# One inference step of a hybrid decoder: the input projection as seven block products

## The chip, the cores and the metric

The kernel runs on one core of one Trainium2 chip. The metric is device microseconds of one execution, from start to end on that core; lower is better. PE is TensorE, DVE is VectorE, ACT is ScalarE, POOL is GpSimd and SP is SyncE, which here only issues DMAs.

## What is computed

One layer on 2048 prompt tokens and 32 sample tokens, width 1024, all in float32. The part that the change touches is the first product, whose result `z` is cut into six column blocks of 512:

```python
h = rms_norm(x, norm_mix_g)                 # (T, 1024)
z = h @ w_in                                # w_in: (1024, 3072)
dq, dk, dv, rq_rk, rv, rg = six blocks of 512 columns of z
dq, dk = partial_rotary(dq) / 8, partial_rotary(dk)      # differential attention
rq, rk = rotate(rq), rotate(rk) / 8                      # retention, chunks of 128 tokens
ret = retention(rq, rk, rv)                 # a state is carried from chunk to chunk
r = silu(rg) * rms_norm(ret)                # per head
```

Differential attention, the output projection, a SwiGLU FFN (width 2816) and a final norm follow. The rotated keys, the values, the retention states and the outputs of the layer are returned.

## The kernel before

Every matmul in full precision is made of three in `float32r`: an operand is split into a high part (a cast on ACT) and a low part (a subtraction on DVE), and high x high, low x high and high x low are added up in PSUM. `split` does this (lines 122 to 124).

`projection` goes over four groups `g` of 512 tokens. For a group it loads x transposed (tiles `xr`, two k-tiles of 128 features each), scales it by the norm's weight into `xh` and `xl`, and adds up squares in `sq` for the norm. Then it goes over the six column blocks in the order 1, 2, 0, 3, 4, 5 (k, v, q, retention's q and k, retention's v, gate). A block's weights come from DRAM as four pieces of 512 KB (`wr`, line 175), each split into `wh` and `wl` (six buffers each). For each of the four tiles of 128 tokens, `terms` issues 8 k-tiles x 3 = 24 matmuls of 128 x 512 into a PSUM bank `z` (lines 295 to 297). ACT and DVE take `z` on: `put_qk` scales, rotates, transposes on PE and splits, and its rows go to DRAM (`q_d`, `k_d`) on POOL's DMA queue; `put_v` stores through SP; block 3 is rotated to `rot`; block 4 starts `retention` of a tile, block 5 the gate and `gated_out`. In group 0 the 32 sample tokens ride along as a fifth tile (`sample_terms`: 16 `float32r` matmuls per block). In group 1 `sample_retention` updates the sample states, with tile `sr`.

The engines run their instructions in program order, and a scheduler sets that order for the whole program while it is built. Tiles of one name take turns in `bufs` buffers; whoever writes one next waits until its last reader is done. The FFN was already computed with seven products in place of eight. After the projection come attention (L793 to L865), the output projection (L952 to L954), `ffn_in` (L1159) and `ffn_out` (L1375).

Of the kernel before, what the change touches and what calls it, by code (L numbers as in the profile page):

```python
# [11 lines left out]
F32 = mybir.dt.float32  # L12
# [9 lines left out]
P = 128  # L22
# [23 lines left out]
class Step:  # L46
# [3 lines left out]
    def run(self):  # L50
        tc = self.tc
        with (
# [10 lines left out]
            ]  # L63
            self.xs_d = dram.tile([P, KT, NS], F32, name="xs_d")
# [78 lines left out]
    def projection(self, const):  # L143
        nc, tc, a = self.nc, self.tc, self.a
        order = (1, 2, 0, 3, 4, 5)
        with (
# [17 lines left out]
            self.state = None  # L164
            for g in range(4):
                tiles = [4 * g + i for i in range(4)] + ([NQ] if g == 0 else [])
                xh, xl = [], []
                wts = {}
                rp = pa.tile([P, 4, 160], F32, tag="rope", name="rope", bufs=2)
                self.rope_t = {4 * g + i: rp[:, i] for i in range(4)}  # L170
                self.rope_t[NQ] = rope_s

                def load_w(b, kp):
                    wr = early.tile([P, 2, 512], F32, tag="wr", name="wr", bufs=2)
                    nc.sync.dma_start(wr, a["w_in"][b, :, 2 * kp : 2 * kp + 2, :])
                    wh = pw.tile([P, 2, 512], F32R, tag="wh", name="wh", bufs=6)
                    wl = pw.tile([P, 2, 512], F32R, tag="wl", name="wl", bufs=6)
                    self.split(wh, wl, wr)
                    wts[b, kp] = (wh, wl)

                sq = early.tile([P, 2, 512], F32, tag="sq", name="sq", bufs=1)
                for kp in range(KT // 2):
                    xr = early.tile([P, 2, 512], F32, tag="xr", name="xr", bufs=2)
                    nc.sync.dma_start(xr, a["xt"][:, 2 * kp : 2 * kp + 2, 512 * g : 512 * g + 512])
                    h = px.tile([P, 2, 512], F32R, tag="xh", name="xh", bufs=5)
                    l = px.tile([P, 2, 512], F32R, tag="xl", name="xl", bufs=5)
                    for j in range(2):
                        gk = gmix[:, 2 * kp + j : 2 * kp + j + 1]
                        nc.scalar.activation(h[:, j], xr[:, j], AF.Copy, scale=gk)  # L189
                        nc.vector.scalar_tensor_tensor(  # L190
                            l[:, j], xr[:, j], gk, h[:, j].bitcast(F32), ALU.mult, ALU.subtract
                        )
                    nc.scalar.activation(sq if kp == 0 else xr, xr, AF.Square)
                    if kp:
                        nc.vector.tensor_tensor(sq, sq, xr, ALU.add)
# [1401 lines left out]
```

## Time and profile before

| | |
|---|---|
| median of 3 runs | 2719.81 us (2718.56 to 2725.04) |
| profiled execution, its own time | 2720.14 us |
| its span, first to last instruction | 2718.4 us |
| mean granted TensorE clock | 0.985 |
| projection | 0 to 679 us of the span |
| groups 0, 1, 2, 3 of it | 0 to 194, to 364, to 522, to 679 us |

The bounds of the groups are read from the timeline: the sums of squares of groups 1, 2 and 3 (`ssp`, L220) stand at 205.5, 375.6 and 533.8 us, some 12 us into a group, and the first scores of attention at 678.9. A row of a group of instructions reads: line, engine, operation, tiles written and read, shape, count | busy us, mean ns of one | idle time of the engine just before them and who ended it. A matmul's duration reaches into the next one; from start to start is what it costs. Times of rows that the prediction uses are shown there.

### The profile page before, as it was taken

The page shows a single profiled execution, that of the slowest core. Times are in us where ns is not written, and L with a number is a line of the kernel's source. Part 1 is how long each engine was busy: PE and PEld are TensorE (multiplying, and loading weights), DVE is VectorE, ACT ScalarE, POOL GpSimd, SP SyncE. Part 2 cuts the span into 40 slices and gives each one's busy share as a digit, 9 for nine tenths or more (in the row PEclk, how much of TensorE's full clock was granted, in tenths as well). Part 3 has the DMA queues.
Part 4 walks back from the last instruction along what each step waited for, and adds up shares of the span by engine and source line. Part 5 has one row for each costly group of instructions (what it writes and reads, how often), then busy time and mean ns, then how long its engine had stood idle before and what let it go on. Part 6 is the DMA issues. An engine that isn't in the chain of part 4 may idle for free.

```text
span 2718.4 us, 35500 instructions
## 1 busy us (share of the span) xinstructions
PE 2624.3 (97%) x13180; PEld 2097.5 (77%) x13180; DVE 1528.1 (56%) x2296; ACT 1065.6 (39%) x2051; POOL 1010.3 (37%) x1032
## 2 busy tenths in 40 slices
PE   8999999999898999998999999999999999999998
PEld 7777788787566788886768777787777777788886
DVE  5554544543556667776365555575766765345364
ACT  4343343432555555654243333353323333333342
POOL 1000000011562233324456555558777784003111
PEclk9999999999899999999999999999999999999999
DMA  7436555364994555624442222354434436744463
GB/s 247 129 102 189 147 156 151 107 180 128 242 249 125 143 158 141 156 79 151 147 171 87 103 101 82 109 174 171 146 129 170 144 131 208 267 142 149 142 207 120
DMA packets 166347, 413.35 MB, mean 152 GB/s; under 512 B 19376, under 2 KB 54896, under 8 KB 164384
## 3 DMA queue, kind: packets, MB, share of 16 engines
q1 hardware_dynamic: 100176, 259.63, 29.5%
q0 software_dynamic: 56784, 147.27, 18.7%
q10 hardware_dynamic: 9216, 4.20, 0.6%
q8 instruction: 104, 1.70, 0.3%
q14 instruction: 67, 0.55, 0.1%
HBM read 287.95 MB, written 123.08 MB: 151 GB/s over the span
## 4 chain that ended last, share of the span: by engine, by line
PE 79%; DVE 7%; DMA 6%; issue 3%; ACT 2%; POOL 2%; ACTq 0%; SPq 0%; POOLq 0%; DVEq 0%
PE fps L1159 22%; PE ops L1375 15%; PE z L297 7%; PE z L295 7%; PE z L296 7%; PE op L851 3%; DVE wl L124 3%; PE sp L793 2%; PE sp L796 2%; PE atp L840 2%; DMA w<-w_ffn_in 2%; PE cz L953 2%; PE cz L952 2%; PE cz L954 1%; DMA w<-w_ffn_out 1%
## 5 line engine op out<-in xcount | busy, mean ns | idle before, releaser
L1159 PE MATMUL fps<-xh,wh 128*128 128x512 f32 x1232 | 484.7, 395 | 4.1 <-ACT xh L123 4.1
L1159 PE MATMUL fps<-xh,wl 128*128 128x512 f32 x1232 | 481.8, 391 | 0.0
L1159 PE MATMUL fps<-xl,wh 128*128 128x512 f32 x1232 | 480.9, 390 | 0.0
L295 PE MATMUL z<-wh,xh 128*128 128x512 f32 x768 | 303.9, 397 | 7.8 <-ACT xh L189 7.8
L297 PE MATMUL z<-wl,xh 128*128 128x512 f32 x768 | 304.1, 397 | 0.0
L296 PE MATMUL z<-wh,xl 128*128 128x512 f32 x768 | 302.6, 394 | 0.0
L1159 PEld LDWEIGHTS fps<-xh,wh 128*128 128x128 f32 x1232 | 231.8, 188 | 70.1 <-issue 14.2
L1159 PEld LDWEIGHTS fps<-xh,wl 128*128 128x128 f32 x1232 | 231.7, 188 | 58.3 <-issue 9.2
L1159 PEld LDWEIGHTS fps<-xl,wh 128*128 128x128 f32 x1232 | 231.9, 188 | 47.1
L124 DVE TENSOR_TENSOR xl<-xl,xh 128x1024 fp32r<-128x1024 f32 (+1 forms) x133 | 149.1, 1144 | 202.0 <-ACT xh L123 201.9
L1375 PE MATMUL ops<-vh,xh 128*128 128x512 f32 x616 | 240.4, 394 | 4.8 <-ACT u L1403 2.6
L1375 PE MATMUL ops<-vh,xl 128*128 128x512 f32 x616 | 239.2, 390 | 0.0
L1375 PE MATMUL ops<-vl,xh 128*128 128x512 f32 x616 | 238.0, 390 | 0.0
L124 DVE TENSOR_TENSOR wl<-w,wh 128x512 fp32r<-128x512 f32 x132 | 158.9, 1220 | 114.9 <-ACT wh L123 114.5
L797 DVE TENSOR_REDUCE mx<-sp 128x1 f32<-128x1024 f32 (+4 forms) x192 | 168.3, 908 | 86.0 <-PE sp L796 65.6
L124 DVE TENSOR_TENSOR wl<-wt,wh 128x512 fp32r<-128x512 f32 x176 | 189.7, 1079 | 30.0 <-ACT wh L123 26.3
L123 ACT CAST xh<-xl 128x1024 fp32r<-128x1024 f32 (+1 forms) x133 | 111.5, 868 | 217.5 <-DMA xl<-hop_d 187.4
L123 ACT CAST wh<-wt 128x512 fp32r<-128x512 f32 x176 | 108.9, 621 | 190.5 <-PE fps L1159 155.6
L124 DVE TENSOR_TENSOR wl<-wr,wh 128x1024 fp32r<-128x1024 f32 x96 | 117.3, 1223 | 109.0 <-ACT wh L123 97.0
L295 PEld LDWEIGHTS z<-wh,xh 128*128 128x128 f32 x768 | 145.1, 189 | 38.0 <-ACT xh L189 7.8
L123 ACT CAST wh<-w 128x512 fp32r<-128x512 f32 x132 | 81.8, 620 | 225.8 <-PE fps L1159 175.0
L297 PEld LDWEIGHTS z<-wl,xh 128*128 128x128 f32 x768 | 144.9, 189 | 31.8 <-issue 0.7
(308 smaller groups left out, 5016.6 us busy)
## 6 DMA issues: line engine op xcount, KB each, us to landing
wr<-w_in SPq DMA_DIRECT2D x96, 512.0 KB
w<-w_ffn_in SPq DMA_DIRECT2D x44, 1024.0 KB
xl<-hop_d SPq DMA_DIRECT2D x77, 512.0 KB
hop_d<-so POOLq DMA_DIRECT2D x88, 256.0 KB
kst<-k_d POOLq DMA_DIRECT2D x36, 512.0 KB
hop_d<-h POOLq DMA_DIRECT2D x66, 256.0 KB
qd<-q_d POOLq DMA_DIRECT2D x64, 256.0 KB
xop_d<-xt POOLq DMA_DIRECT2D x56, 256.0 KB
```

The costliest lines, as they stand in the source:

```text
L123: nc.scalar.copy(hi, src)
L124: nc.vector.tensor_tensor(lo, src, hi.bitcast(F32), ALU.subtract)
L295: mm(z, h[:, j, c], wh[:, j], start=k == 0, stop=False)
L296: mm(z, l[:, j, c], wh[:, j], start=False, stop=False)
L297: mm(z, h[:, j, c], wl[:, j], start=False, stop=k == KT - 1)
L793: nc.tensor.matmul(sp[:, o : o + nn], q[:, 2 * mp, sl], k, start=True, stop=False)
L796: nc.tensor.matmul(sp[:, o : o + nn], q[:, 2 * mp + 1, sl], k, start=False, stop=True)
L797: nc.vector.tensor_reduce(mx[:, c : c + 1], sp[:, :w], AX.X, ALU.max, negate=True)
L840: nc.tensor.transpose(tp[:, j, :], pt[b // 8][0][:, P * (b % 8) : P * (b % 8) + P], self.ident)
L851: self.nc.tensor.matmul(st["o"], ats[(b - lo) // 4][:, (b - lo) % 4, :], vs[b // 4][:, b % 4, :], start=b == 0, stop=b == st["i"],)
L1159: i = nc.tensor.matmul(bank, w[:, c], v, start=first and k == 0 and n == 0, stop=k == half - 1 and n == 2, skip_group_check=True,)
L1375: nc.tensor.matmul(bank, x[:, c], w, start=first and n == 0, stop=end and n == 2, skip_group_check=True)
```

## The change

The input projection is computed with one level of Strassen's scheme (seven products of half size in place of eight). A group's x (512 tokens x 1024 features) is a 2 x 2 matrix of blocks: tokens in halves of 256, features in halves of four k-tiles. The weights of two column blocks (`pairs`: 1 with 2, 0 with 3, 4 with 5) are the other 2 x 2 matrix: the same halves of features, and the two blocks. A `product` is two token tiles x 4 k-tiles x 3 = 24 matmuls of 128 x 512.

- x: `xr` now holds k-tile k and k + 4. DVE scales it in place; `a` (the two blocks a11 and a12, for products 0 and 1) and `b` (a22, product 3) are split off; POOL forms four sums in place; `c` (products 5 and 2) and `d` (products 6 and 4) are split from them. Each of the eight operand tiles has one buffer.
- Weights: products 0, 1 and 2 read `w_in` as before. Products 4, 3, 6 and 5 read four sums of weight blocks from a new DRAM tensor `tin_d`, straight into the buffer of `wl`, where ACT and DVE split them.
- `prepare` makes these sums, in group 0 only: for each pair, k-tile k and half of the columns it loads four blocks of 128 x 256 into `wq` (two buffers), uses them at once for the sample tokens (fp32 matmuls with 32 rows, the four blocks on four strips of the bank `zsp`), then POOL subtracts four times in place and stores the four results to `tin_d`. That is 24 such chunks of 512 KB. `prepare` for the first pair stands ahead of the products, for the next pairs behind product 1 of the pair before.
- Results: products 0, 5 and 4 are kept (`u`, `v`), and DVE adds them to the other products out of PSUM (`f`), POOL makes one more sum per pair of tiles. `put` takes on what the loop's branches did before. A pair's products run in the order 0, 1, 5, 4, 2, 6, 3.
- To make room in SBUF: `wh`, `wl` five buffers for six, `qkh`, `qkl` 256 tokens for 512, `vrow`, `rt`, `sm`, `rope` and `sr` one buffer for two, `ro` three for four.

```diff
+            self.tin_d = [dram.tile([P, 4, KT // 2, 512], F32, name=f"tin_d{p}") for p in range(3)]
...
-        order = (1, 2, 0, 3, 4, 5)
+        pairs = ((1, 2), (0, 3), (4, 5))
+        half = KT // 2
...
+            where = {0: ("a", 0), 1: ("a", 1), 3: ("b", 0), 5: ("c", 0), 2: ("c", 1), 6: ("d", 0), 4: ("d", 1)}
+            def weights(bp, o, wts):
+                b, c = pairs[bp]
+                for k in (0, 2):
+                    h = pw.tile([P, 2, 512], F32R, tag="wh", name="wh", bufs=5)
+                    l = pw.tile([P, 2, 512], F32R, tag="wl", name="wl", bufs=5)
+                    if o < 3:
+                        i = k + (half if o else 0)
+                        src = a["w_in"][c if o == 2 else b, :, i : i + 2, :]
+                    else:
+                        src = self.tin_d[bp][:, {4: 0, 3: 1, 6: 2, 5: 3}[o], k : k + 2, :]
+                    r = early.tile([P, 2, 512], F32, tag="wr", name="wr", bufs=2) if o < 3 else l.bitcast(F32)
+                    nc.sync.dma_start(r, src)
+                    self.split(h, l, r)
+                    wts[o, k // 2] = (h, l)
...
+            def prepare(sap, xs, bp):
+                b, c = pairs[bp]
+                z = ps.tile([P, 512], F32, tag="r", name="zsp", bufs=2)
+                for k in range(half):
+                    for n in range(2):
+                        cols = slice(256 * n, 256 * n + 256)
+                        w = sap.tile([P, 2, 2, 256], F32, tag="wq", name="wq", bufs=2)
+                        for e in range(2):
+                            nc.sync.dma_start(w[:, e], a["w_in"][pairs[bp][e], :, k : k + half + 1 : half, cols])
+                        for e in range(2):
+                            for i in range(2):
+                                q = 2 * e + i
+                                nc.tensor.matmul(
+                                    z[32 * q : 32 * q + 32, cols],
+                                    xs[:, k + half * i, :],
+                                    w[:, e, i, :],
...
+                        w11, w21, w12, w22 = w[:, 0, 0], w[:, 0, 1], w[:, 1, 0], w[:, 1, 1]
+                        padd(w11, w12, w11, ALU.subtract)
+                        padd(w12, w22, w12, ALU.subtract)
+                        padd(w22, w22, w11, ALU.subtract)
+                        padd(w21, w21, w22, ALU.subtract)
+                        nc.gpsimd.dma_start(
+                            self.tin_d[bp][:, :, k, cols], w.rearrange("p e i c -> p (e i) c")
+                        )
...
+                for n, m in (("a", 2), ("b", 1), ("c", 2), ("d", 2)):
+                    x[n] = [px.tile([P, m, half, 256], F32R, tag=f"x{i}{n}", name=f"x{i}{n}") for i in "hl"]
+                for k in range(half):
+                    xr = load_x(g, k)
...
+                    xh, xl = x["a"]
+                    self.split(xh[:, :, k], xl[:, :, k], xr[:, :, :256])
+                    a11, a21, a12, a22 = xr[:, 0, :256], xr[:, 0, 256:], xr[:, 1, :256], xr[:, 1, 256:]
+                    xh, xl = x["b"]
+                    self.split(xh[:, 0, k], xl[:, 0, k], a22)
+                    padd(a22, a21, a22, ALU.add)
+                    padd(a21, a11, a21, ALU.subtract)
+                    padd(a11, a22, a11, ALU.subtract)
+                    padd(a12, a12, a11, ALU.subtract)
+                    for n, cols in (("c", slice(0, 256)), ("d", slice(256, 512))):
+                        xh, xl = x[n]
+                        self.split(xh[:, :, k], xl[:, :, k], xr[:, :, cols])
...
+                    for p in range(2):
+                        product(0, p, z[p], x, wts, True, False)
+                        u.append(line("u", 2))
+                        nc.scalar.copy(u[p], z[p])
...
+                        product(1, p, z[p], x, wts, False, True)
+                        out(b, p, z[p])
+                    if g == 0 and bp < 2:
+                        zsn = prepare(sap, xs, bp + 1)
+                    weights(bp, 5, wts)
...
+                        product(3, p, z[p], x, wts, False, True)
+                        f = line("f", 2)
+                        add(f, z[p], u[p], ALU.add)
+                        out(b, 2 + p, f)
...
-        vr = self.early.tile([P, 512], F32, tag="vrow", name="vrow", bufs=2)
+        vr = self.early.tile([P, 512], F32, tag="vrow", name="vrow", bufs=1)
...
-            sr = pool.tile([P, NH, P], F32, tag="sr", name="sr", bufs=2)
+            sr = pool.tile([P, NH, P], F32, tag="sr", name="sr", bufs=1)
```

How it moves the instructions, at three places. A row of the order has line, operation, tiles written and read, shape, and what it waits for (DMAHW: a DMA that SP issued, DMASW: one that POOL issued, else an engine).

PE, group 0, where the first column block's tiles end (before): the sample tile (`xs`) follows on weights that are in SBUF already, and the next block's first tile after it.

```order
L307 MATMUL z_514<-wh_307,xs_318 64x512
L308 MATMUL z_514<-wl_308,xs_318 64x512
L307 MATMUL z_514<-wh_307,xs_318 64x512
L308 MATMUL z_514<-wl_308,xs_318 64x512
L295 MATMUL z_572<-wh_550,xh_249 128x512 [waits Activation_49]
L296 MATMUL z_572<-wh_550,xl_250 128x512
L297 MATMUL z_572<-wl_551,xh_249 128x512
L295 MATMUL z_572<-wh_550,xh_249 128x512
```

PE, group 0, first pair (after), ahead of the second half of product 5 (`wh_688`): `wq_587` and `wq_599` are the first two chunks of the second pair.

```order
L218 MATMUL zsp_586<-wq_587,xsr_372 32x256
L218 MATMUL zsp_586<-wq_599,xsr_372 32x256 [waits DMAHW2_49]
L218 MATMUL zsp_586<-wq_599,xsr_372 32x256
L218 MATMUL zsp_586<-wq_599,xsr_372 32x256 [waits DMAHW3_49]
L218 MATMUL zsp_586<-wq_599,xsr_372 32x256
L197 MATMUL z_693<-wh_688,xhc_253 128x512 [waits Activation_49]
L197 MATMUL z_693<-wh_688,xlc_254 128x512
L197 MATMUL z_707<-wh_688,xhc_253 128x512
L197 MATMUL z_707<-wh_688,xlc_254 128x512
L197 MATMUL z_693<-wl_689,xhc_253 128x512 [waits DVE_49]
```

Where weights in SBUF were all that PE took, it now stands behind a strip matmul for each load of a chunk.

SP, first DMAs of group 0 (before): x and weights, each behind a buffer that ACT and DVE have read.

```order
L175 DMA wr_289<-w_in 128x1024 [waits DMAHW1_49,DVE_49]
L184 DMA xr_279<-xt 128x2x512 [waits DMAHW0_49,DVE_49]
L175 DMA wr_305<-w_in 128x1024 [waits DMAHW3_49,DVE_49]
L184 DMA xr_295<-xt 128x2x512 [waits DVE_49]
L175 DMA wr_548<-w_in 128x1024 [waits DMAHW5_49,DVE_49]
L175 DMA wr_554<-w_in 128x1024 [waits DMAHW7_49,DMAHW2_49,DVE_49]
```

SP, group 0 (after): `wl_684` and `wl_689` are the two halves of product 5's weights, `wq_*` chunks of `prepare`.

```order
L214 DMA wq_438<-w_in 128x2x256 [waits DMAHW2_49,DMAHW1_49,DMASW5_49]
L214 DMA wq_438<-w_in 128x2x256
L186 DMA wl_684<-tin_d0_89 128x1024 [waits DMAHW3_49]
L214 DMA wq_450<-w_in 128x2x256 [waits DMAHW5_49,DMAHW4_49,DMAHW6_49,DMASW2_49,Pool_49]
L214 DMA wq_450<-w_in 128x2x256
L214 DMA wq_462<-w_in 128x2x256 [waits DMAHW1_49,DMAHW2_49,DMASW3_49,Pool_49]
L214 DMA wq_462<-w_in 128x2x256 [waits DMAHW7_49]
L214 DMA wq_587<-w_in 128x2x256 [waits DMAHW4_49,DMAHW0_49,DMAHW5_49,DMASW4_49,Pool_49]
L214 DMA wq_587<-w_in 128x2x256
L214 DMA wq_599<-w_in 128x2x256 [waits DMAHW6_49,DMAHW7_49,DMASW5_49,Pool_49]
L214 DMA wq_599<-w_in 128x2x256 [waits DMAHW3_49]
L186 DMA wl_689<-tin_d0_89 128x1024 [waits PE_49]
```

Loads of chunks now wait for POOL and for earlier stores from its queue (DMASW), and the reads of `tin_d` are queued behind them.

DVE, end of a group and begin of the next (before, groups 0 to 1): x of the next group is split beside the last rows of the sample tile.

```order
L190 SCALAR_TENSOR_TENSOR xl_1685<-xr_1682,gmix_179,xh_1684 128x512 [waits DMAHW5_49,Activation_49]
L373 SCALAR_TENSOR_TENSOR ro_1402<-ro_1402,rss_1597,gate_1595 128x128 [waits Pool_49]
L373 SCALAR_TENSOR_TENSOR ro_1402<-ro_1402,rss_1597,gate_1595 128x128 [waits DVE_49]
L373 SCALAR_TENSOR_TENSOR ro_1402<-ro_1402,rss_1597,gate_1595 128x128 x2
L190 SCALAR_TENSOR_TENSOR xl_1685<-xr_1682,gmix_179,xh_1684 128x512 [waits Activation_49]
L190 SCALAR_TENSOR_TENSOR xl_3005<-xr_3002,gmix_179,xh_3004 128x512 [waits DMAHW6_49,Activation_49]
L312 TENSOR_TENSOR zs_1627<-z_1610,zs_1627 32x512 [waits DVE_49]
L190 SCALAR_TENSOR_TENSOR xl_3005<-xr_3002,gmix_179,xh_3004 128x512 [waits Activation_49]
L462 TENSOR_TENSOR skd_1920<-rot_s_216,sdec_1889 32x4x64 [waits DMAHW3_49]
L462 TENSOR_TENSOR skd_1920<-rot_s_216,sdec_1889 32x4x64
L124 TENSOR_TENSOR wl_2041<-wr_2038,wh_2040 128x1024 [waits DMAHW7_49,Activation_49]
```

DVE, the same place (after, groups 2 to 3): `f_4772` is the last eviction of product 3, `xlb_4832` the first write to the `b` operand of the next group.

```order
L394 TENSOR_TENSOR f_4772<-z_4637,u_4368 128x512 [waits PE_49,Pool_49]
L125 TENSOR_TENSOR xlb_4832<-xr_4838,xhb_4831 128x256 [waits Activation_49]
L125 TENSOR_TENSOR xlb_4832<-xr_4871,xhb_4831 128x256 [waits Activation_49]
L119 TENSOR_SCALAR rss_4623<-rss_4623 128x4 [waits Activation_49]
L492 TENSOR_TENSOR sm_4715<-sp_4716,rmask_244 128x2x128 [waits DVE_49,PE_49]
L492 TENSOR_TENSOR sm_4715<-sp_4717,rmask_244 128x2x128 [waits PE_49]
L522 TENSOR_TENSOR ro_4744<-op_4724,rdec_246 128x2x128 [waits PE_49]
L125 TENSOR_TENSOR wl_5052<-wl_5052,wh_5051 128x1024 [waits DMAHW1_49,Activation_49]
L472 SCALAR_TENSOR_TENSOR ro_4485<-ro_4485,rss_4623,gate_4621 128x128 [waits Pool_49]
L472 SCALAR_TENSOR_TENSOR ro_4485<-ro_4485,rss_4623,gate_4621 128x128 [waits DVE_49]
```

The rest of the x operands of group 3 follows over the next 36 rows, up to the `xla` of k-tile 3, with retention of the last two tiles between them. Before, the buffers of x let its split run ahead of the last matmuls; now `b`, `c` and `d` come behind them.

More of the change, by code (lines that the diff above doesn't have):

```diff
@@ L165, in projection @@
             for g in range(4):
[L166 to L169, printed above, removed]
+                wts, x = {}, {}
+                rp = pa.tile([P, 4, 160], F32, tag="rope", name="rope", bufs=1)
                 self.rope_t = {4 * g + i: rp[:, i] for i in range(4)}
                 self.rope_t[NQ] = rope_s
[L173 to L179, printed above, removed]
```

242 lines of the change are left out of this document (136 added, 106 removed).

## The prediction

> **What bounds the kernel now.** I read the page first (engine shares), then the busy time by stage, the groups of instructions of the projection, and last the timeline at single places.
>
> ```profile
> span 2718.4 us, 35500 instructions
> PE 2624.3 (97%) x13180; PEld 2097.5 (77%) x13180; DVE 1528.1 (56%) x2296; ACT 1065.6 (39%) x2051; POOL 1010.3 (37%) x1032
> ```
>
> The same profiled execution took 2720.14 us, so 1.7 us lie outside its span; the median of the three runs is 2719.81. The sum below starts from 2720.1. The projection is all of the change. Its four token groups are four stretches of the span (columns: us, then busy us of PE, PEld, DVE, ACT, POOL, the granted clock, the DMA share, GB/s):
>
> ```profile
> 0.00:194.00 194.00, 186.23 (x893) 145.64 (x894) 99.20 (x194) 80.55 (x134) 20.59 (x33) 0.99 0.51 155
> 194.00:364.00 170.00, 169.54 (x847) 135.16 (x846) 88.81 (x191) 61.30 (x104) 13.23 (x18) 1.00 0.55 163
> 364.00:522.00 158.00, 158.00 (x769) 127.71 (x768) 74.46 (x146) 60.87 (x104) 12.58 (x17) 1.00 0.50 146
> 522.00:679.00 157.00, 157.00 (x770) 126.43 (x768) 64.14 (x134) 48.51 (x93) 21.53 (x31) 1.00 0.54 150
> ```
>
> PE is busy throughout and nothing else is near full. One idle stretch of 7.8 us stands at the start, before the first operands:
>
> ```profile
> L295 PE MATMUL z<-wh,xh 128*128 128x512 f32 x768 | 303.9, 397 | 7.8 <-ACT xh L189 7.8
> 201.39 0.39 PE L295 MATMUL z<-wh,xh 128*128 128x512 f32 x1
> 202.07 0.39 PE L295 MATMUL z<-wh,xh 128*128 128x512 f32 x1
> ```
>
> The 397 ns overlap. From 201.39 to 202.07 there are three matmuls (L295, L296, L297), so one costs 0.227 us of PE. Per group 6 blocks x 4 tiles x 8 k x 3 = 576 of them are 131 us of the 158; 27 us are transposes and retention.
>
> **What comes off PE.** Seven products of 24 matmuls replace 192 per pair: 72 fewer per group, 288 in all, 288 x 0.227 = -65.4 us (16.3 per group). The 96 sample matmuls (L307, L308) become 96 fp32 ones of 32 x 256 on strips. The same form stands in the FFN:
>
> ```profile
> L307 PE MATMUL z<-wh,xs 128*64 128x512 f32 x48 | 19.0, 396 | 0.0
> 1383.99 1.05 PE L1204 MATMUL sz<-w,xs 128*32 128x256 f32 x10
> 1384.97 0.73 PE L1159 MATMUL fps<-xh,wh 128*128 128x512 f32 x2
> ```
>
> Ten records, two to an instruction, hold PE for 0.98 us: 0.2 each, 19 us against 96 x 0.227 = 22, so -3. Half of the 32 ssp matmuls go: under -2. Gross gain 70 us, at most.
>
> **Group 0: the sums kept in DRAM.** Products 5, 4, 6 and 3 read sums that this same group must first write. `prepare` makes 24 chunks (three pairs, eight each), and a chunk's buffer goes round: two loads on SP, four strip matmuls, four dependent POOL subtractions of 256 columns, a store on POOL's queue; with two buffers the next load waits until a store has landed. The order shows the strip matmuls of the following chunks on PE ahead of product 5's second half, and SP's read of the sums behind those loads. Prices:
>
> ```profile
> 66.49 1.47 SPq L175 DMA_DIRECT2D wr<-w_in  x2
> 70.53 1.05 ACT L123 CAST wh<-wr 128x1024 fp32r<-128x1024 f32 x1 [0.87 <-DMA wr<-w_in]
> 257.66 4.17 DMA ret_sample<-sr
> 261.84 4.35 DMA sr<-state_ret
> 1300.86 0.76 POOL L1001 DMA_DIRECT2D xop_d<-xt  x1 [4.33 <-DVE xt L987]
> 1304.05 1.28 POOL L1013 TENSOR_TENSOR xt<-xt 128x512 f32<-128x512 f32 x1 [2.43 <-DMA xop_d<-xt]
> L1323 POOL TENSOR_TENSOR wt<-w 128x512 f32<-128x512 f32 x11 | 14.0, 1273 | 44.1 <-DMA w<-w_ffn_out 44.1
> L1144 POOL TENSOR_TENSOR wt<-w 128x512 f32<-128x512 f32 x44 | 69.9, 1606 | 3.9 <-DVE wl L124 3.9
> ```
>
> A 512 KB load is used 4.0 us after its issue. A 256 KB store is waited for 4.17 us (issued by SP) or 3.2 us (by POOL: 1300.86 to 1304.05); I take 3.5 for 512 KB, nearer to the POOL row, since POOL issues these. POOL's 256 columns were not run; half of 1.27 and of 1.61 bounds them by 0.64 and 0.80, I take 0.71. Both buffers go in step (POOL alternates between them), so two chunks cost 3.5 + 4.0 + 0.5 (strip matmuls) + 8 x 0.71 = 13.7 us, with bounds of 12.1 and 15.1 (POOL 0.64 and 0.80, store 3.2 and 4.17, load 4.0 and 4.35). Twelve such rounds are 164 us. The first chunk lands near 10, and some 14 us are added where POOL does the sums of x (16 x 0.71, half of it beside a landing) and stands behind the stores of q and k. The last sum is in DRAM near 188. Then 4.0 for its read, 2.3 for cast and split, and 108 matmuls (half of product 5, then 4, 2, 6, 3) of 24.5 us: group 0 ends near 219, 2 more for matmuls in the slow clock (below): 221 against 194, **+27**. By the bounds -6 to +44: 19 down and 17 up for the rounds, 14 down if all the added POOL work is hidden.
>
> The DMA queues give a second bound. Group 0 moved 194 us x 155 GB/s = 30 MB. Added are 9.4 MB of weights (42 half-megabyte loads for 24), 12.6 MB of chunk loads and 12.6 of stores: 65 MB.
>
> ```profile
> DMA packets 4337, 8.76 MB, mean 274 GB/s; under 512 B 1472, under 2 KB 1488, under 8 KB 4336
> ```
>
> That is the first 32 us, the densest stretch of the projection. 65 MB at 274 GB/s are 236 us, so a group 0 much under 200 is not to be had from this side either.
>
> After a wait PE is slow for a while:
>
> ```profile
> 1376.08 1.22 PE L1159 MATMUL fps<-xh,wh 128*128 128x512 f32 x2 [4.09 <-ACT xh L123]
> 1378.80 0.63 PE L1159 MATMUL fps<-xh,wh 128*128 128x512 f32 x1
> 1379.23 0.63 PE L1159 MATMUL fps<-xl,wh 128*128 128x512 f32 x1
> 1380.01 0.39 PE L1159 MATMUL fps<-xh,wh 128*128 128x512 f32 x1
> ```
>
> After 4.09 us idle a matmul takes 0.43 until 1379.66, then 0.23: some eight at +0.2, 1.6 us a gap. In group 0 most gaps end in another wait on the chain, which takes that up; I count one gap, 2 us. (The Trainium skill, "TensorE: Matmul & The Clock Gate", Part 1, speaks against the change here: after an idle window of about 3.4 us PE drops to half its clock and needs as much busy time to come back. The row agrees. If each of some eight gaps were paid in full, an estimate by that rule, the sum would be 12 us more than mine.)
>
> **Groups 1 to 3: the boundary.** Here the sums lie ready and PE has 141 us of work (158 - 16.3 - 0.6). DVE's rows:
>
> ```profile
> L124 DVE TENSOR_TENSOR wl<-wr,wh 128x1024 fp32r<-128x1024 f32 x96 | 117.3, 1223 | 109.0 <-ACT wh L123 97.0 <-DMA v_prompt<-vrow 11.5
> L385 DVE COPY rt<-tp 128x512 f32<-128x512 f32 x16 | 11.0, 687 | 3.6 <-PE tp L383 3.3
> L190 DVE SCALAR_TENSOR_TENSOR xl<-xr,gmix,xh 128x512 fp32r<-128x512 f32 x32 | 22.7, 745 | 2.7 <-ACT xh L189 2.7
> L195 DVE TENSOR_TENSOR sq<-sq,xr 128x1024 f32<-128x1024 f32 x12 | 14.6, 1218 | 0.2
> L601 DVE TENSOR_SCALAR dpr<-dpr,dk 128x544 f32<-128x544 f32 x2 | 1.0, 520 | 0.0
> L373 DVE SCALAR_TENSOR_TENSOR ro<-ro,rss,gate 128x128 f32<-128x128 f32 x64 | 18.2, 347 | 20.0 <-ACT gate L280 15.2 <-POOL rss L119 4.7
> L393 DVE TENSOR_TENSOR sm<-sp,rmask 128x256 f32<-128x256 f32 x32 | 13.2, 422 | 36.1 <-PE sp L391 36.1
> L415 DVE SCALAR_TENSOR_TENSOR state<-state,rdec,up 128x128 f32<-128x128 f32 x30 | 9.0, 342 | 1.1 <-PE up L409 1.1
> ```
>
> Per group 18 more splits of 1.22 (22), 24 adds out of PSUM at 0.69 (17), and for x some 19 instead of 8 x 0.745 + 3 x 1.22 = 10: +48, on about 80 (the four stretches' mean): 128 us, under PE's 141. It is not the sum that hurts but one place. The x operands have one buffer, so the next group's b operand (read by product 3, the last) is written only after the last matmul, then POOL makes c and d, then the two x buffers come free and k = 2 and 3 are loaded. The order has 50 DVE rows between the last eviction and the xla of k = 3: 3 weight splits (3.7), 12 gated rows (4.2), 8 of the sm kind (3.4), 4 states (1.4), 12 of 128x512 (8.3), 4 scalings (2.0), 3 xlb (1.3), 4 small ones (0.6): 25 us. PE has there the retention of two tiles, one of them
>
> ```profile
> 674.33 0.71 PE L391 MATMUL sp<-rt 64*128 64x128 f32 x4
> 678.89 0.38 PE L793 MATMUL sp<-kst,qd 128*128 128x256 f32 x1
> ```
>
> 4.6 us long (the next work begins at 678.89), and 18 matmuls of products 5 and 0 (4.1): 13 us. **+12** per boundary; the bounds are 0 (DVE's retention work slips behind) and +16 (its waits for ACT and DMA in between). Before, PE had 158.00 of 158 there.
>
> Small edits: five weight buffers for six, `vrow` one for two (the second v tile's eviction holds ACT until two stores have landed, some 4 us, with half a product, 2.7 us, of cover), one `rt`, one `sm`, three `ro`, two u, v and f each. The cover is the one and a half products (8 us) between a weight buffer's release and its use; a load, cast and split take 4.0 + 1.05 + 1.22. Thin: 0 to 8 us a group, taken as 3. `sr` with one buffer makes the sample states serial (4.17 + 4.35 + work, four times, some 43 us) beside a pair of 41 us of PE: 0 to 6, taken as 2. ACT gains 18 casts of 1.05 and 12 copies, some 35 us on 61: covered.
>
> Sum: +27, then 3 x (-16.9 + 12 + 3) = -6, +2: +23. 2720.1 + 23 = **2743**.
>
> **Rivals.** (1) Quick rounds: 12.1 us each (POOL 0.64, landings of 3.2 and 4.0). Group 0 ends near 202, +8; with -6 and +2, 2724: no change. For it: the POOL store row; against it: two DMA streams beside it. (The Trainium skill, "DMA: Bandwidth & Descriptors", "Anatomy of one DMA", puts a POOL-issued DMA at 2.0 us plus bytes over 436 GB/s, an estimate of 3.2 us for 512 KB: it is on this side; the 4.17 us row is above it.) (2) Faster: with quick rounds, DVE's retention rows slip behind the x operands and a boundary costs 2 and not 12. Group 0 +8, then 3 x (-16.9 + 2 + 3) = -36, and +2: 2694. It decides from boundaries under about 7 us. (3) Much slower: the DMA bound rules group 0, 236 us, +42, and the boundaries cost 16: 2720 + 42 + 6 + 2 = 2770. (4) PE is not the bound in the projection, so fewer matmuls give nothing: excluded by 158.00 of 158.
>
> **How the numbers follow.** Forecast 0.48, (1) 0.14, (2) 0.20, (3) 0.18. Within 0.3% (8 us) is what a measurement of this kernel can hardly tell from no change. Slower 0.66, same 0.14, faster 0.20. The range leaves a tenth on either side: 2692, just past (2), and 2785, past (3) by the clock's 12. Of the likeliest case alone: 2728 to 2760.
>
> **What would show it.** The ssp matmuls of group 1, at 205.5 now, come near 235; the waits name DMA wq and tin_d for PE, ACT and POOL, some 50 us of PE idle before 221. At three boundaries DVE is solid for 25 us and PE idle for 12. In between a product takes 24 x 0.227 = 5.45 us. Wrong would be: group 0 under 200, or boundaries with PE full.

## The result, and the profile after

The changed kernel took 2853.32 us in its profiled execution, 2853 to 2863 in its runs, against 2719.2 us (median) of the kernel before: a ratio of 1.0501, interval 1.0471 to 1.0531. One more run, in which the granted clock was 0.645 and not 0.947, took 3739 us and is not counted. I had predicted 2743; slower was right, by 133 us and not by 23.

The page of the changed kernel: span, busy time, and the granted clock in 40 slices of 71 us.

```profile
span 2851.5 us, 36218 instructions
PE 2637.2 (92%) x12956; PEld 2071.1 (73%) x12956; DVE 1745.0 (61%) x2543; ACT 1174.3 (41%) x2218; POOL 1229.5 (43%) x1256
PEclk7787898998979999999999999999999999999999
```

PE has 224 matmul instructions fewer and is busy 13 us *longer*. The last row tells where: in the first twelve slices, 855 us and with them the projection, the clock was down to 0.7 or 0.8 in eight, and it was at 0.9 or more in all that follow. Busy time by stage, cut at the ssp matmuls of groups 0 to 3 (their marks) and at the first attention matmul, with group 0 in three pieces, first of the changed kernel, then three of the same stretches of the kernel before (us, then busy us of PE, PEld, DVE, ACT, POOL, the granted clock, DMA share, GB/s):

```profile
0.00:42.00 42.00, 14.26 (x50) 6.22 (x50) 25.59 (x40) 16.91 (x27) 28.82 (x39) 0.80 0.69 225
42.00:125.00 83.00, 56.63 (x235) 35.80 (x236) 36.42 (x46) 22.50 (x30) 49.45 (x59) 0.69 0.68 223
125.00:246.00 121.00, 88.60 (x395) 60.24 (x394) 73.78 (x107) 39.82 (x60) 65.80 (x76) 0.81 0.74 229
246.00:318.80 72.80, 62.91 (x251) 46.45 (x250) 50.91 (x93) 33.81 (x70) 19.58 (x16) 0.76 0.46 150
318.80:491.80 173.00, 164.80 (x770) 128.21 (x768) 131.82 (x238) 87.92 (x148) 43.73 (x46) 0.94 0.63 199
491.80:657.00 165.20, 151.86 (x698) 117.96 (x698) 126.23 (x217) 87.54 (x153) 39.28 (x43) 0.94 0.63 201
657.00:815.00 158.00, 146.12 (x659) 114.36 (x658) 105.40 (x181) 72.39 (x122) 50.84 (x58) 0.92 0.75 219
```

```profile
0.00:28.50 28.50, 20.73 (x84) 17.06 (x85) 18.92 (x30) 18.78 (x24) 6.32 (x15) 1.00 0.86 283
28.50:205.50 177.00, 177.00 (x861) 138.09 (x861) 89.33 (x179) 66.88 (x115) 14.27 (x18) 0.99 0.47 140
533.80:678.90 145.10, 145.10 (x712) 116.85 (x710) 55.85 (x121) 42.53 (x78) 20.52 (x30) 1.00 0.55 151
```

Start +13.6 (42.1 for 28.5), group 0 from mark to mark +99.7 (276.7 for 177.0), groups 1 to 3 +2.9, +7.0 and +13.0: together 136 us, and nothing behind the projection. Group 0 is most of the loss; groups 1 to 3 lose where each should have gained 16.9.

What group 0 waits for (engine, waited for: us, times, longest; to 318.8 us):

```profile
ACT wh L124 <- DMA wl<-tin_d: 92.9, 22, 28.7
POOL wq L227 <- PE zsp L218: 43.7, 10, 7.2
PE zsp L218 <- DMA wq<-w_in: 41.8, 12, 9.7
SPq L214 <- DMA tin_d<-wq: 92.5, 14, 14.9
```

The longest of these, in the chain of work around it (start, us, what; rows left out are marked):

```profile
74.85 4.06 DMA wq<-w_in
...
78.95 2.77 PE zsp L218 x12
...
81.75 0.72 POOL wq L227
...
85.83 0.77 POOL wq L230
86.60 0.29 issue
86.89 3.44 DMA tin_d<-wq
...
91.62 5.83 DMA wl<-tin_d
...
97.48 1.05 ACT wh L124
...
98.58 11.17 PE z L197 x36
109.75 0.57 PE zsp L218 x8
```

That is one round of two chunks: load 4.06, strips 2.8 (at a granted clock of 0.50), POOL 5.1, store 3.44, then the next loads on SP: 15.5 us. Only then does SP issue the reads of the sums (91.62), which stood behind the chunk loads. The next strips wait behind 36 matmuls of the products (98.58 to 109.75), and POOL's subtractions with them. So it goes on to the end of group 0: the stores, SP's wait for the last of them, the reads behind it, and the last matmul of the last product.

```profile
L231 POOL DMA_DIRECT2D tin_d<-wq x24: 695/728/837, 28.8 to 242.6; - x24
SPq L186 <- DMA tin_d<-wq: 19.8, 1, 19.8
246.00 1.28 SPq L186 DMA_DIRECT2D wl<-tin_d  x3
289.49 0.39 PE L197 MATMUL z<-wl,xhb 128*128 128x512 f32 x1
```

The last of the 24 stores is issued at 242.6 and has landed at 246.0, where the forecast had 188: 19 us a round. Group 0's last product ends at 289.9.

### The profile page after: what moved, and what is told of

It reads as the page before. It is cut to its first block, busy times and chain, and to the rows that moved or that the text cites. A ratio compares the mean times of both kernels' runs of the same rounds, so it can differ in the third digit from the quotient of the medians.

```text
span 2851.5 us, 36218 instructions
## 1 busy us (share of the span) xinstructions
PE 2637.2 (92%) x12956; PEld 2071.1 (73%) x12956; DVE 1745.0 (61%) x2543; ACT 1174.3 (41%) x2218; POOL 1229.5 (43%) x1256
## 4 chain that ended last, share of the span: by engine, by line
PE 67%; DMA 12%; DVE 10%; ACT 4%; issue 4%; POOL 2%; SPq 0%; ACTq 0%; POOLq 0%; DVEq 0%
PE fps L1258 25%; PE ops L1474 14%; PE z L197 7%; DMA wl<-tin_d 4%; PE op L950 3%; DVE wl L125 3%; PE sp L892 2%; PE sp L895 2%; PE atp L939 2%; PE cz L1051 2%; PE cz L1052 2%; PE cz L1053 2%; ACT wh L124 1%; DMA w<-w_ffn_in 1%; DMA xr<-xt 1%
## 5 line engine op out<-in xcount | busy, mean ns | idle before, releaser
L125 DVE TENSOR_TENSOR wl<-wl,wh 128x1024 fp32r<-128x1024 f32 x96 | 124.1, 1295 | 129.3 <-ACT wh L124 128.1
L124 ACT CAST wh<-wl 128x1024 fp32r<-128x1024 f32 x96 | 100.6, 1048 | 188.7 <-DMA wl<-tin_d 187.6
L892 PE MATMUL sp<-kst,qd 128*128 128x512 f32 (+1 forms) x320 | 127.9, 400 | 27.0 <-ACT p L910 25.8
L950 PE MATMUL op<-vv,at 128*128 128x128 f32 x1088 | 142.4, 279 | 0.3 <-ACT at L941 0.3
L1474 PEld LDWEIGHTS ops<-vh,xh 128*128 128x128 f32 x616 | 116.1, 189 | 31.0 <-ACT u L1502 4.0
L950 PEld LDWEIGHTS op<-vv,at 128*128 128x128 f32 x1088 | 133.0, 194 | 4.7 <-issue 2.5
```

The lines of the kernel that those rows point to most:

```text
L124: nc.scalar.copy(hi, src)
L125: nc.vector.tensor_tensor(lo, src, hi.bitcast(F32), ALU.subtract)
L892: nc.tensor.matmul(sp[:, o : o + nn], q[:, 2 * mp, sl], k, start=True, stop=False)
L950: self.nc.tensor.matmul(st["o"], ats[(b - lo) // 4][:, (b - lo) % 4, :], vs[b // 4][:, b % 4, :], start=b == 0, stop=b == st["i"],)
L1474: nc.tensor.matmul(bank, x[:, c], w, start=first and n == 0, stop=end and n == 2, skip_group_check=True)
```

## Experiments

One profiled run each, beside the kernel before (2715 to 2725 us). Differences are taken from the changed kernel's 2853.3; its own runs reach from there to 2862.9, so under 10 us is not read from a total. A run's mark is the place of group 1's ssp matmuls (318.8 in the changed kernel), its periods are the times from there to the next marks and to the attention (496.3 together). Where a kernel leaves work out, its expectation says which.

**Group 0.** Reads of a tile that is always ready:

```diff
+ self.alt_d = dram.tile([P, 2, 512], F32, name="alt_d")
+ self.nc.gpsimd.dma_start(self.alt_d, self.a["w_in"][0, :, 0:2, :])
  src = self.tin_d[bp][:, {4: 0, 3: 1, 6: 2, 5: 3}[o], k : k + 2, :]
+ src = self.alt_d if g == 0 else src
```

> In group 0 the products 3 to 6 read one fixed 512 KB tile in DRAM, written once at the start, and not the sums of prepare (their values are wrong); prepare itself, its loads, strips, subtractions and stores, is as before. Theory A (the sums' way through DRAM sets the end of group 0): the reads no longer wait, group 1's ssp matmuls come 60 to 80 us earlier than the 318.8 us of the changed kernel, and the time falls to about 2785. Theory B (the strip matmuls stand in PE's order ahead of products that are ready, so PE waits for chunk loads whoever reads the sums): under 20 us earlier, 2840 to 2855. Theory C (the bytes set it): no change, 2853.

Measured 2778.8 (-75); group 1's ssp at 253.5. Theory A, and most of the loss.

```diff
- for e in range(2):
+ for e in range(2 if k == 0 else 0):
      for i in range(2):
```

> The strip matmuls run for the first two of the eight chunks of a pair only (the sample rows are wrong), everything else as in the changed kernel. Theory A: the last sum still has to come through its 24 rounds, the strips were a short link of each; 10 to 25 us less, about 2835. Theory B: PE is free of the chunk loads, the 41.8 us of waits at the strips go with the slow matmuls behind them; 45 us or more less, under 2810. Theory C: no change, 2853.

Measured 2824.1 (-29), ssp at 298.3. This lies between the two, nearer to A's 10 to 25: the strips are a link of the round, and a longer one than A had said.

Both edits at once:

> Both edits to group 0 at once: products 3 to 6 of group 0 read the fixed tile, and the strips run for two chunks of eight (sample rows and products wrong). PE is free of prepare, which goes on loading, subtracting and storing beside it. If waiting alone was the loss of group 0: group 1's ssp at 210 to 222, as without any sums (216.5). If the traffic of the loads and stores, or their place in SP's queue, costs by itself: 230 to 245.

Measured 2779.8, ssp at 234.0: in the total no better than the first edit alone, though the mark came 20 us earlier. Prepare did not get quicker; its stores were issued from the first to

```profile
L234 POOL DMA_DIRECT2D tin_d<-wq x24: 713/745/842, 33.4 to 288.5; - x24
```

that is, into group 1, which reads the sums, and there the time that group 0 had won was given back (ssp to ssp 191 us; 161 with the first edit alone). SP's queue points to why: up to 290 us it stood at weight loads whose buffer DVE (46.6 us) or PE (43.9 us) had not yet read out, and 39.3 us at stores of chunks, and the loads of chunks stood behind both.

```diff
- padd(w11, w12, w11, ALU.subtract)
...
- nc.gpsimd.dma_start(self.tin_d[bp][:, :, k, cols], ...)
- src = self.tin_d[bp][...]
+ src = self.alt_d
```

> prepare keeps its loads and its strips, but makes no sums and no stores; products 3 to 6 of all groups read one fixed 512 KB tile in DRAM (values wrong). Theories A and B: a chunk's buffer comes free when its four strips are done, two chunks take a load's 4 to 5 us and not 19, so both the reads and the strips stop waiting; group 1's ssp near 225 to 240 instead of 318.8, the time about 2765 to 2775. Theory C: 12.6 MB of some 65 are gone, a fifth; group 0 some 50 us shorter at most, 2800 or more. Groups 1 to 3 keep their 496 us from the ssp marks of group 1 to the attention in all theories.

Measured 2731.2 (-122), ssp at 216.5; groups 1 to 3 took 486 us. More than expected: making the sums, even where group 0's products do not wait for them, still costs some 48 us (2779.8 - 2731.2). How that divides into store traffic, POOL's time, SP's queue and the reads of groups 1 to 3 was not measured. And without any sums the kernel is still 11 us slower than before.

SP's queue by itself, the loads moved to POOL's:

```diff
- nc.sync.dma_start(w[:, e], a["w_in"][pairs[bp][e], ...])
+ nc.gpsimd.dma_start(w[:, e], a["w_in"][pairs[bp][e], ...])
```

> The changed kernel with the chunk loads of prepare issued on POOL's queue and not on SP's, so that the weight and x loads no longer stand behind a chunk load that waits for a store to land (92.5 us of SP's waits in group 0). Theory G (this place in SP's queue is what made a round 19 and not 13.7 us): group 1's ssp matmuls 25 to 45 us earlier than 318.8, the time 2810 to 2830. Theory A alone (load, subtractions, store and the dependent read are each slower with the traffic): within 10 us of 318.8, or later where POOL now stands still for the landing.

Measured 2882.5 (+29), ssp at 341.9. Theory G is not borne out: the wait for the landing only moved, and POOL now stood still for it (18.5 us at the loads), with its subtractions behind. A queue in which nothing else stands was not tried.

Sums made beside eight block products:

```diff
+ if g == 0:  # per block: two token pairs x 8 k x 3, samples with split weights
+     ...
+     for _ in range(3):
+         next(chunks, None)
```

> Group 0 makes its eight block products as the kernel before did (token pairs of 2 x 128, samples with the fp32r split weights), and prepare, without strips, writes the sums beside it; groups 1 to 3 as in the changed kernel. Nothing in group 0 waits for a sum. Theories A and B: PE has the 186 us of work it had before, group 1's ssp near 215 to 235, the time about 2755 to 2775: all that is left above 2720 are the boundaries and stalls of groups 1 to 3. Theory C: 55 MB in group 0 slow the weight loads; group 1's ssp at 260 or later, 2800 or more.

Measured 2767.2 (-86), ssp at 238.5; 498 us for groups 1 to 3. The time is as theories A and B said, group 0 3.5 us over their range.

**The boundaries of groups 1 to 3.** The changed kernel from group 1 to 2: the last matmul on b, then the x operands (start, us, engine, line, operation; a choice of the rows):

```profile
461.30 0.40 PE L197 MATMUL z<-wl,xhb 128*128 128x512 f32 x1
463.81 1.53 POOL L295 TENSOR_TENSOR xr<-xr 128x256 f32<-128x256 f32 x2 [6.46 <-DVE xlb L125]
472.06 1.55 POOL L298 TENSOR_TENSOR xr<-xr 128x256 f32<-128x256 f32 x2
474.68 1.28 DVE L125 TENSOR_TENSOR xlc<-xr,xhc 128x512 fp32r<-128x512 f32 x2
475.39 1.21 SPq L172 DMA_DIRECT2D xr<-xt  x2
479.71 0.63 ACT L284 ACTIVATE s<-xr 128x512 f32<-128x512 f32 x1 [0.97 <-DMA xr<-xt]
486.75 0.69 DVE L125 TENSOR_TENSOR xla<-xr,xha 128x512 fp32r<-128x512 f32 x1
493.52 0.68 DVE L125 TENSOR_TENSOR xla<-xr,xha 128x512 fp32r<-128x512 f32 x1
```

32.5 us from the end of product 3 to the last xla: 9.8 are POOL's sums (463.8 to 473.6), 4.3 the landing of two late loads. Which link counts was tried one at a time.

```diff
+ if g == 2:  # pool pb, opened where the sample states were
+     x["b"] = [pbp.tile([P, 1, half, 256], F32R, name=f"y{i}b") for i in "hl"]
```

> The changed kernel with a second buffer for the x operand b (a22) of group 2, so that at the boundaries 1 to 2 and 2 to 3 the next group's b is split while product 3, the last, still runs. Theory D (the boundary's chain: b free, four sums on POOL, c and d, x buffers free, two more x loads): the chain starts 5 us or more earlier at two boundaries; the periods from the ssp matmuls of group 1 to the attention, 496 us now, fall by 14 to 24, the time to 2830 to 2840. Theory E (DVE is simply full there, or the slow matmuls after the gap are what is lost): under 6 us, 2848 to 2858.

Measured 2846.7; periods 495.8. No gain. At boundary 1 to 2 the split still came at 462.5, since its space was the sample states', in use until then; 2 to 3 won 6 us, as much as the first lost.

```diff
+ if g and k == 1:  # 32 matmuls on xhb, xha into a spare bank
+     nc.tensor.matmul(zw, x["a"][0][:, 0, 0, :P], x["b"][0][:, 0, :2]..., ...)
```

> The changed kernel with 32 more matmuls of 128x512 at each of the three boundaries (on the next group's first operands, into a bank that nobody reads), 7.3 us of PE at full clock each, so that PE is busy where it waited. Theory F (the slow clock after the gaps is itself on the path at the boundaries, some 8 us each): the products behind run at 0.23 and the three periods end no later, 496 or up to 10 us less. Theory D (the x operands' chain sets the boundary, slow matmuls lie beside it): 0 to 7 us more per boundary, 496 to 515, although the granted clock there goes up.

Measured 2844.4; periods 503.0. The first 7.3 us of fillers stand ahead of group 1's mark, which came at 312.0, 6.8 us *earlier*. There, at boundary 0 to 1, they held the clock (the changed kernel, then this run):

```profile
290.00:332.00 42.00, 32.72 (x121) 24.45 (x121) 31.58 (x58) 20.86 (x45) 19.18 (x19) 0.67 0.43 139
290.00:332.00 42.00, 41.91 (x205) 32.48 (x206) 36.44 (x67) 24.92 (x51) 21.87 (x19) 1.00 0.57 183
```

At boundary 1 to 2 the clock stayed at 1.00 until 470 and fell to 0.50 from 476 to 488 all the same. The projection ended at 815.1, as in the changed kernel: 22 us of matmuls were added, all of them fitted into time that was lost anyway, and nothing was won. This does not decide between F and D. At the first boundary, by the mark, the slow clock was on the path, as F says; at the second the fillers only put it off, and the periods, 7 us longer, are as D says.

```diff
- pairs = ((1, 2), (0, 3), (4, 5))
+ pairs = ((0, 3), (4, 5), (1, 2))
```

> The changed kernel with the pairs in the order (0, 3), (4, 5), (1, 2): retention and gates come in the middle pair, and a group ends with the k and v tiles. Theory H (at a group's end two tiles of retention go to and fro between PE and DVE, and their DVE rows stand among those of the next x operands): the periods from the ssp matmuls of group 1 to the attention, 496 us now, fall by 18 to 30. Theory D (the x operands' own chain of sums, buffers and loads sets the boundary): they fall by less than 8, and group 0 is where it was in both, 319 within 10.

Measured 2875.6 (+22); projection end at 853.9 for 815.0. The periods grew to 546 us, so theory H falls, as a whole; that k and v now come last, right ahead of the attention, is part of this run too.

With this order in groups 1 and 2 only, the buffer for b, and the sample states moved to the start of group 1:

> The changed kernel with the three edits to groups 1 to 3 alone: the pair order (0, 3), (4, 5), (1, 2) in groups 1 and 2, the second buffer for b of group 2, the sample states at the start of group 1. Group 0 is untouched. If the boundaries were what groups 1 to 3 lost: the 496 us fall to 455 to 470 and the time to 2820 to 2835, with group 1's ssp at 319 within 10; group 0's share of the loss, 113 us, stays whole. If they do not fall by 15, the shorter groups belong to the other group 0.

Measured 2846.8; periods 490.6, group 1's ssp at 323.4. No gain that can be told.

```diff
- if k + i:
-     add(sq, sq, s, ALU.add)
...
- nc.vector.scalar_tensor_tensor(o[:m, h], o[:m, h], ss[:m, h : h + 1], gt[...], ...)
```

> The changed kernel without seven of the eight additions of squares per group (7 x 0.69) and without the gating products of the retention rows (16 x 0.35), both on DVE, some 10 us of DVE per group, most of it at the boundary (row scales and outputs are wrong). Theory E (DVE is what is full at a boundary): the three periods from group 1's ssp to the attention, 496 us, fall by 18 to 30. Theory D (the x chain's waits for buffers, POOL and loads): by less than 9.

Measured 2844.9. The ssp matmuls no longer wait for sums and come early, so the marks don't compare; the projection ended at 820.9, not earlier than 815.0. The total moved by 8 us where theory E had 18 to 30: DVE's full slices are not the bound.

```diff
+ if g:
+     continue  # groups 1 to 3: no x load, no sums, no splits
  xr = load_x(g, k)
```

> The changed kernel with the x operands and the sum of squares made in group 0 only; groups 1 to 3 use group 0's (values wrong) and load and split no x. If the x operands, by their chain or by their 28 us of DVE a group, are what groups 1 to 3 lost, the 496 us come near PE's own work, 51 less than the 473 of the kernel before: 425 to 445. If the retention at a group's end or the single buffers of the small tiles are, they stay above 470.

Measured 2783.6 (-70); the projection ended at 752.3, 63 earlier. The marks move here too, so the expected 425 to 445 cannot be read. The x operands, with their loads, sums and splits, are what the boundaries cost, 21 to 23 us each.

```diff
+ pool = pbp if g > 1 and k > 1 else early
- xr = early.tile([P, 2, 512], F32, tag="xr", name="xr", bufs=2)
+ xr = pool.tile([P, 2, 512], F32, tag="xr", name="xr", bufs=2)
```

> The changed kernel with two more x buffers for k = 2 and 3 of groups 2 and 3 (in the space of the sample states, which move to the start of group 1), so that at the boundaries 1 to 2 and 2 to 3 all four x loads can land before the last product ends. The run without x operands gave 70 us for three boundaries, 23 each. If the two late loads of each (issued when c of k = 0 and 1 is split, landed 4 to 5 us later, then squared, scaled and split) are the long part: 8 to 14 at each of the two boundaries, 2825 to 2838. If POOL's four sums in a row and the splits behind them are: under 4 each, 2845 to 2855.

Measured 2839.2 (-14), a microsecond off the first range; periods 156.4, 156.2 and 171.1, together 483.7 for 496.3. The boundary 1 to 2 (columns as above), first as changed, where product 3 ends at 461.7, then with the two buffers, where b is split 12 us later, at 473.7:

```profile
464.00:470.00 6.00, 4.38 (x26) 2.80 (x24) 4.68 (x9) 4.34 (x9) 6.00 (x6) 0.97 0.12 48
470.00:476.00 6.00, 4.78 (x16) 3.31 (x14) 6.00 (x15) 3.68 (x10) 4.62 (x5) 0.50 0.11 44
476.00:482.00 6.00, 6.00 (x16) 4.46 (x16) 3.09 (x9) 2.39 (x5) 0.00 (x0) 0.50 0.66 218
```

```profile
476.00:482.00 6.00, 6.00 (x33) 4.83 (x32) 6.00 (x9) 4.75 (x10) 6.00 (x6) 1.00 0.84 287
482.00:488.00 6.00, 6.00 (x31) 4.71 (x31) 6.00 (x10) 3.49 (x5) 6.00 (x7) 1.00 0.14 57
488.00:494.00 6.00, 4.54 (x21) 3.20 (x21) 6.00 (x11) 4.88 (x9) 5.10 (x6) 1.00 0.30 91
```

Here the late loads were the long part: PE is full but for 1.5 us and the clock never falls. Some of it may belong to the sample states, which had to move for the space. The boundary 2 to 3 still had a slice at 0.50 (648 to 654), and the last period grew from 158 to 171, so the total won little. What is left of the 23 us I put down to POOL's sums and the splits; no run shows it.

**Towards a faster version.** Four kernels with eight products in group 0 and the chunk loads on POOL's queue:

> Eight block products in group 0 with the sums made beside it, chunk loads on POOL's queue, and the second buffer for b of group 2. From the hybrid's 2767: group 0, which had 33 us above the kernel before, gets 10 to 20 back when no weight load stands behind a waiting chunk, and two boundaries 7 to 12 each: 2725 to 2745. It beats 2720 only if both come at their upper end and a boundary gives more than 12.

Measured 2763.8: group 0 won 10 us from mark to mark (34.7 to 230.9), groups 1 to 3 only 4 (494 for 498). That misses the 2725 to 2745 by the boundaries, expected to give 7 to 12 each.

> Eight block products in group 0 with the sums made beside it, chunk loads on POOL's queue, a second buffer for b of group 2, the sample states at the start of group 1 so that this buffer is free in time, and the pair order of the run with the middle retention. From 2764: theory H gives 15 to 25 more and the buffer some 5: 2735 to 2745. If only theory D holds, 2755 to 2765. Under 2720, faster than both kernels, would need more than the boundaries that these traces show.

Measured 2765.9. Groups 1 and 2 took 148 and 155 us from mark to mark, but group 1's mark came at 263, and with k and v last PE was busy for some half of the time or less from 714 to 744, ahead of the attention.

> As the run with all changes, but only groups 1 and 2 have the pairs in the order (0, 3), (4, 5), (1, 2); groups 0 and 3 keep (1, 2), (0, 3), (4, 5). Theory H, with the order harmful where k and v come last before something that needs their stores (the attention; POOL's queue in group 0): group 0 ends near 231, groups 1 and 2 take 148 to 158 each, group 3 near 155, attention near 690, the time 2725 to 2740. If what shortened groups 1 and 2 there was only that group 0 had ended late and left less behind: they take 165 or more, 2755 or more.

Measured 2773.9: group 1's mark at 272.9, groups 148, 162 and 157 us. The short groups began late.

> Eight block products in group 0 with the sums made beside it, chunk loads on POOL's queue, and the two more x buffers. From 2764 by the same 16 to 28 as the run beside it, if the late loads are the long part: 2736 to 2748; else 2756 to 2764. Not faster than 2720 in either case.

Measured 2767.8, above both ranges, with group 1's mark at 270.3. This run keeps the order of the pairs. So in all three kernels with the sample states at the start of group 1 the mark came at 263 to 273, where it stood at 230.9 without, in either order: the short groups are at least in part a mark that moved. No version here beats the kernel before.

**Both causes out.**

> Both removed together: prepare makes no sums and no stores (products 3 to 6 of all groups read the fixed tile), and the x operands are made in group 0 only (values wrong in both). By themselves these took 122 and 70 us off the changed kernel's 2853. If they are all of the loss and independent: 2853 - 122 - 70 = 2661, within 12, which is the kernel before less 59 of the 70 us that the missing matmuls are worth. If the retention at the ends of groups or the small single buffers hold a loss of their own behind them: 2680 or more.

Measured 2691.3, 24 under the kernel before beside it (2715.2) and 30 over the 2661 of independent parts. So there is a third loss, or the two are not independent; the run does not tell how much is which. Some 13 us stand at the start: two waits that neither edit touches,

```profile
PE z L199 <- ACT xha L126: 14.1, 1, 14.1
PE z L199 <- ACT wh L126: 8.9, 1, 8.9
```

where the kernel before waited once, 7.8 us; group 0's ssp matmuls come at 41.6 here and at 42.1 in the changed kernel, for 28.5 before. Another part shows at the projection's end, where the pair (4, 5) leaves two tiles of retention behind the last product (the last 30 us of the projection, the changed kernel, then before):

```profile
785.00:815.00 30.00, 27.40 (x118) 19.74 (x117) 18.14 (x46) 7.13 (x28) 14.94 (x14) 0.70 0.62 198
```

```profile
649.00:679.00 30.00, 30.00 (x157) 22.73 (x155) 9.46 (x29) 6.29 (x22) 2.03 (x2) 1.00 0.38 112
```

With both causes out the granted clock of the last 30 us is still 0.73. How much that end costs was not measured by itself.

## Why the prediction was right in sign and wrong in size

- **What bounds the kernel, and -70 of PE work**: borne out as far as it can be seen; with both causes out the kernel is 24 us under before, and PE is full in most of its slices.
- **"Group 0: the sums kept in DRAM", +27.** This term failed. The last product of group 0 ended at 289.9 where 221 was forecast: 69 of the 110 us by which the sum is short. *Rounds of 13.7* account for 58 (the last sum in DRAM at 246.0, not 188). Three parts were priced nearly right (load 4.06 for 4.0, store 3.44 for 3.5, POOL 5.1 for 5.7); the strips, called 0.5 us a round, took 2.8 in the clean one, and leaving out three quarters of them was worth 29 us. But the step that failed is that the four were put end to end as if nothing else stood in the same queues. Measured were 15.5 us in a clean round and 19 in the mean: POOL waited 43.7 us for strips that stood behind products in PE's order, SP 92.5 us at chunk loads. The prediction names the strips in PE's order and the reads behind the chunk loads in SP's queue, and prices neither wait. Its bounds are also added up wrongly: its own prices make 12.8 and 15.4 us a round, not 12.1 and 15.1, and with 12.8 the quick rounds of rival (1) end group 0 near 211 and not 202. *The tail of 31 us* after the last sum took 44, at a granted clock of 0.82.
- **"2 more for matmuls in the slow clock".** Wrong as a count: the granted clock was 0.69 to 0.81 all through group 0. (The Trainium skill, "TensorE: Matmul & The Clock Gate", Part 1, by whose rule I had estimated 12 us more, agrees with group 0 in kind: after 4.1 us without a matmul, 74.8 to 78.9, the clock is 0.50. At boundary 1 to 2 it fell without such a wait, as the last section shows.) What the clock costs beside the waits was not separated in group 0. Fillers held it at 1.00 at boundary 0 to 1 and put its fall off at the next; over all three they paid for themselves and won nothing. With the late loads on time it did not fall at 1 to 2.
- **"+12 per boundary".** The mechanism was right as far as the runs show it: b, POOL's sums, two x buffers, late loads. The size was not: 21 to 23 us. I took DVE's 25 us as the length of the chain less 13 us of cover; it was 32.5, since POOL's 9.8 us and the 4.3 us landing lie in it and not beside it, and a part of the cover ran at half clock. Less DVE work gave nothing that can be told, so DVE was the wrong engine to count. PE also did not sit idle for 12 us, as "what would show it" said: it is busy for 4.4 to 6.0 of 6 us, from 470 on at half clock.
- **Groups 1 to 3, -6 in all**: +23 between the marks, +40 from the last product of group 0 (525 us to the attention, for 485), which is the count that goes with the 69 above. Three boundaries at 10 more than priced are 30 of the remaining 41 us; the projection's end had no term of its own.
- **Rivals.** All three end below what was measured. Quick rounds would have needed 12 to 13 us, and the clean one took 15.5. The DMA bound (236 us, 274 GB/s) was not it: group 0 moved 223 to 229 GB/s up to 246 us, and the edit that only frees the reads kept all the bytes and took off 75. The faster rival needed boundaries under 7 us.

## What to carry to other kernels

A product that reads what the same stage has just made in DRAM pays for every queue that the making passes, in order: price the round with the other work that stands in those queues, not as a sum of durations (here 19 us and not 13.7). Before saving matmuls, look at what the operands of the next stage wait for; saving a tenth of PE's work also shortens the time in which loads and splits are hidden. And read PE's busy share together with the granted clock: at boundary 1 to 2 PE counted as busy for 6.00 of 6 us at a clock of 0.50.

## What the runs showed that I had not expected

- The clock fell without a long gap. At boundary 1 to 2 of the changed kernel it went to 0.50 at 469.6; the longest idle time of PE in the 8 us ahead was 1.30 us, but from 461.6 on PE had only the short fp32 matmuls of retention. And it fell and stayed down while PE was full of those (the run with two more x buffers, the projection's end):

```profile
792.00:798.00 6.00, 5.84 (x27) 4.30 (x26) 3.57 (x12) 2.22 (x9) 3.84 (x4) 0.52 0.51 146
798.00:804.00 6.00, 6.00 (x19) 4.20 (x18) 2.40 (x9) 0.40 (x2) 4.65 (x5) 0.50 0.98 360
```

  Twelve microseconds of a PE that counts as busy did not bring the clock back. In the kernel before, such matmuls stood among the products and the clock was 1.00. That their kind is the cause is not shown by a run of its own.
- A chunk pipeline that group 0 did not wait for did not run faster: its last store was issued at 288.5 with most strips gone and no product of group 0 reading the sums, against 242.6 where they did. SP's waits point to the place of its loads in SP's queue; no run tested that by itself.
- A mark inside a pipeline moves when its own inputs come earlier: with two more x buffers the first two periods were 26 us shorter (156.4 and 156.2 for 173.0 and 165.2), and the projection ended only 9 us earlier. Its end is such a mark too: with the pairs in another order it came 39 us later and the total only 22. The total is the measure.
